# Loading the two rotary tables of a streaming encoder layer one sample sooner

## The chip, the cores and the metric

The kernel runs on one core of one Trainium2 chip. The metric is the time of one execution in device microseconds (us); lower is better. The engines are TensorE (PE in the rows, its weight loads PEld), VectorE (DVE), ScalarE (ACT), GpSimd (POOL) and SyncE (SP); SP and POOL do no arithmetic here, their instruction queues issue the transfers.

## The reference

One layer of a hybrid encoder is applied to a prompt of 512 frames and to 8 samples of 16 new frames each, with one set of weights. In order:

```python
x = x + 0.5 * swiglu(rms_norm(x, g1), w_in1, w_out1)
h = rms_norm(x, g_mix)
z = h @ w_in_mix            # rq rk rv rg | fq fk fv ff | two merge gates
q, k = rotary(rq, pos), rotary(rk, pos) * DK ** -0.5
o_ret = rms_norm(retention(q, k, rv, state)) * silu(rg)
o_fox = forgetting_attention(fq, fk, fv, log_sigmoid(ff), cache)
x = x + (g0 * (o_ret @ w_br_ret) + g1 * (o_fox @ w_br_fox)) @ w_out
x = x + 0.5 * swiglu(rms_norm(x, g2), w_in2, w_out2)
x = x + (p @ w_ple) * sigmoid(rms_norm(x, g_ple) @ w_ple_gate)
```

Each sample attends to 1024 cached frames of keys and values. The retention has 4 heads with keys of 128 and values of 256. `rotary` turns each pair of halves of a key or query by an angle that depends on its position:

```python
x1, x2 = xf[..., :half], xf[..., half:]
return concat([x1 * c - x2 * s, x1 * s + x2 * c])
```

## The kernel before

All 640 tokens (512 of the prompt, 128 of the samples) are kept with features on the 128 partitions and tokens along the free dimension. Weights arrive as raw f32 tiles (`raw`, 1 MB) and are split by `Parts.add` into a rounded part `wh` (ScalarE, line 282) and the rest `wl` (VectorE, line 283); three matmuls of 320 columns per weight block make up an f32 product (`mm`, line 205).

In the middle stage the input projection of the mixer is run as a list of units (`run_units`), and this work is the filler between the steps of the attention and of the retention: `fill(us)` lets the units go on for that much modelled matmul time. A unit of kind "s" (`MixSeven`) makes two blocks of 128 channels with seven products in three banks of PSUM, a, b and c (`pa`, `pg`, `pg`). Between its products, `after` combines the banks: after the third product VectorE subtracts a copy of bank a from bank b (line 819) and ScalarE copies bank b out (line 820), and only then may the fifth product write bank b again; VectorE subtracts that copy from bank c (line 824).

The main program around the change runs the eight samples one after the other (class `Sample`): their cached keys and values are loaded by `Sample.load` into tiles `kv` of 1 MB, of which there are four. The values of a sample are summed in `Sample.values`, one matmul group for each half of the cache (`pa<-kv,att`), scaled by VectorE at line 1335 and folded by a matmul (line 205, `pa<-sm,tmp`, copied out at line 1342). Behind the last sample come four heads of the retention (class `Retention`). `first_loads` and `loads` fetch a head's keys and queries from the scratch tensor `zdram` in DRAM, twice, once with the halves exchanged, six transfers for a head. They go into the `kv` tiles that the values of the seventh sample occupied, so they can't be issued before these are summed up. `rotate(0)` and `rotate(1)` then do the rotation for keys and queries with the two tables `tab`: two multiplications with the cosines and the sines (lines 1374 and 1375) and an addition (line 1376) each, on VectorE, over 640 columns.

The order in which instructions stand on each engine isn't the order of the program text. A scheduler sets it from its own model of how long things take; every engine then works off its row in order. Transfers issued by `load` go through the queue of SP, in that order too, and each of them also waits until the eighth one before it on that queue has landed. `load` itself is held back only by a scheduling hint: no sooner than `lead` of modelled matmul time before the place in the text.

The two tables are 128x640 in f32, 320 KB each, in `blk` tiles. Before the change they are loaded behind the last sample, after `until("rk")`, `fill(FILL_B)` and `pump(True)`.

Of the kernel before, what the change touches and what calls it, by code (L numbers as in the profile page):

```python
# [23 lines left out]
NB = 8  # L24
# [107 lines left out]
def kernel(  # L132
# [20 lines left out]
    def nm(base):  # L153
        uid[0] += 1
        return f"{base}_{uid[0]}"
# [3 lines left out]
    def blk(shape=(P, T), dt=F32, tag="blk"):  # L159
        n = 1  # L160
        for s in shape[1:]:
            n *= s
        assert n <= T
        return bp.tile(list(shape), dt, tag=tag, name=nm(tag), bufs=slots[tag])
# [16 lines left out]
    def tmp(shape=(P, H2), dt=F32):  # L181
        return bp.tile(list(shape), dt, tag="tmp", name=nm("tmp"), bufs=NTMP)
# [26 lines left out]
    def after(inst, name, why):  # L209
        tc.add_manual_dep(inst.ins, name, mybir.DependencyInfo(mybir.DependencyClass.NoSync, mybir.DependencyReason.SCHED_ONLY), reason=why)  # L210

    def load(out, in_, lead=LEAD):

        i = nc.sync.dma_start(out, in_)  # L214
        at = clock[0] - lead
        name = next((nm_ for c, nm_ in reversed(issued) if c <= at), None)
        if name is not None:
            after(i, name, "no tile taken too soon")
# [433 lines left out]
    with tc.manual_schedule(engines={mybir.EngineType.SP}):  # L652
        for q in range(KC // 2):
            cols = slice(q * 256, (q + 1) * 256)
            xi = big((P, TB, 256))
            n = P if q == 0 else 256
# [103 lines left out]
    def defer(us, thunk):  # L760
        uid[0] += 1
        heapq.heappush(deferred, (clock[0] + us, uid[0], thunk))

    def pump(everything=False):
        while deferred and (everything or deferred[0][0] <= clock[0]):
            heapq.heappop(deferred)[2]()
# [828 lines left out]
    def fill(us):  # L1595
        credit[0] += us
        while credit[0] > 0.0:
            at = clock[0]
            if next(feed, feed) is feed:
                clock[0] += credit[0]  # L1600
                credit[0] = 0.0
            credit[0] -= clock[0] - at
            pump()
# [24 lines left out]
    samples[0].load(samples[0].k, cache_k)  # L1628
    samples[0].load(samples[0].k, cache_k)
    fill(FILL_B)  # L1630
    for b in range(NB):
        defer(2.0, lambda: samples[b].loads(samples[b + 1] if b + 1 < NB else None))
        for n in range(8):
            samples[b].step(n)
            fill((FILL_S if b else FILL_S0) / 8)
    until("rk")
    fill(FILL_B)
    pump(True)
    tab = []
    for n in range(2):  # L1640
        r = blk()
        load(r, c_rope[n])
        tab.append(r)
    gqt, smt = tmp([P, RH, 2, 2 * L]), blk([P, RH, P])
    load(gqt, c_gq)
    load(smt, c_smask)
# [26 lines left out]
    for op in range(KC // 2):  # L1673
# [5 lines left out]
        for o in range(2):  # L1679
            n = 2 * op + o  # L1680
# [114 lines left out]
```

## Time and profile before

| | |
|---|---|
| median of 3 runs | 1624.56 us (1623.99 to 1625.74) |
| the profiled execution | 1622.67 us, its span 1620.9 us |
| TensorE busy | 1609.3 us, 99% of the span |
| VectorE / ScalarE busy | 1164.4 us (72%) / 731.5 us (45%) |
| mean granted clock of TensorE | 0.998 of full speed |

The profiled execution is 1.77 us longer than its span, which begins at its first instruction; it lies 1.9 us under the median of the runs. Since TensorE is busy nearly all the time, a change shows in the time where TensorE stands still, or where its clock is low, for longer or shorter than before. 0.2% of the time is 3.2 us.

### The profile page before, as it was taken

How to read it: one execution, taken by the hardware profiler on the slowest of the kernel's cores; microseconds unless marked ns; L12 is line 12 of the kernel's file. 1: busy time of each engine (PE TensorE's matmuls, PEld its weight loads, DVE VectorE, ACT ScalarE, POOL GpSimd, SP SyncE). 2: the span in 40 equal slices, each digit the busy share in tenths (PEclk: the TensorE clock that was granted, in tenths of full speed). 3: DMA queues.
4: the chain of work that ended last, by engine and by line, in shares of the span. 5: the costliest groups of instructions: out<-in, count | busy, mean ns of one | idle time of the engine just before them, and what ended most of it. 6: DMA issues, size and time to landing. Idle time of an engine off the chain costs nothing.

```text
span 1620.9 us, 30289 instructions
## 1 busy us (share of the span) xinstructions
PE 1609.3 (99%) x11979; PEld 1557.3 (96%) x11979; DVE 1164.4 (72%) x2472; ACT 731.5 (45%) x1536; POOL 94.5 (6%) x172
## 2 busy tenths in 40 slices
PE   9999999999999999999999999999999999999998
PEld 8999999999999888988889999999999999999998
DVE  6885786577777755777779886558884787578663
ACT  6552354244454444444434454435653355235432
POOL 0000000000011111000000010001000000000000
PEclk9999999999999999999999999999999999999999
DMA  7244233433542333577775676444234333433431
GB/s 249 78 131 139 96 93 131 145 101 94 178 130 97 111 115 133 209 281 269 279 259 179 202 260 247 151 135 155 79 101 164 100 91 124 144 111 90 172 123 46
DMA packets 205566, 242.88 MB, mean 150 GB/s; under 512 B 10176, under 2 KB 175984, under 8 KB 201328
## 3 DMA queue, kind: packets, MB, share of 16 engines
q1 hardware_dynamic: 193824, 200.07, 38.0%
q0 software_dynamic: 11392, 40.79, 6.3%
q8 instruction: 94, 1.54, 0.4%
q14 instruction: 48, 0.39, 0.1%
q10 hardware_dynamic: 208, 0.08, 0.0%
HBM read 194.89 MB, written 46.03 MB: 149 GB/s over the span
## 4 chain that ended last, share of the span: by engine, by line
PE 96%; DMA 2%; DVE 1%; ACT 1%; issue 0%; SPq 0%; DVEq 0%
PE pa L205 74%; PE pg L205 18%; PE pa L228 4%; DMA kv<-zdram 1%; DMA blk<-in_c_rope_dram 0%; DMA raw<-in_ffn_w_in_dram 0%; ACT tmp L533 0%; PE pg L228 0%; DVE wl L283 0%; ACT wh L282 0%; DMA kv<-in_x_prompt_dram 0%; SPq L214 0%; DVE kv L1487 0%; ACT blk L361 0%; DVE blk L1473 0%
## 5 line engine op out<-in xcount | busy, mean ns | idle before, releaser
L282 ACT CAST wh<-raw 128x512 fp32r<-128x512 f32 (+1 forms) x525 | 316.3, 613 | 506.7 <-PE pa L205 323.5
L205 PE MATMUL pa<-blk,wh 128*128 128x320 f32 x2344 | 511.1, 311 | 1.1 <-ACT wh L282 1.0
L283 DVE TENSOR_TENSOR wl<-raw,wh 128x512 fp32r<-128x512 f32 (+1 forms) x525 | 351.0, 678 | 107.0 <-ACT wh L282 103.6
L205 PEld LDWEIGHTS pa<-blk,wh 128*128 128x128 f32 x2344 | 388.2, 189 | 4.5 <-ACT wh L282 1.5
L205 PE MATMUL pa<-blk,wl 128*128 128x320 f32 x1172 | 344.4, 310 | 0.0
L205 PE MATMUL pa<-kv,wh 128*128 128x320 f32 x1344 | 251.5, 308 | 0.0
L205 PEld LDWEIGHTS pa<-blk,wl 128*128 128x128 f32 x1172 | 216.5, 189 | 0.5 <-DVE blk L830 0.4
L205 PEld LDWEIGHTS pa<-kv,wh 128*128 128x128 f32 x1344 | 210.6, 188 | 0.0
L205 PE MATMUL pg<-blk,wh 128*128 128x320 f32 x768 | 177.3, 316 | 0.2 <-DVE blk L830 0.2
L205 PE MATMUL pa<-blk,blk 128*128 128x320 f32 (+2 forms) x1064 | 168.3, 304 | 0.0
L205 PE MATMUL pa<-kv,wl 128*128 128x320 f32 x672 | 154.6, 308 | 0.0
L205 PEld LDWEIGHTS pa<-blk,blk 128*128 128x128 f32 (+1 forms) x1064 | 151.9, 183 | 0.1
L205 PE MATMUL pg<-wh,blk 128*128 128x256 f32 x768 | 147.6, 286 | 0.0
L205 PEld LDWEIGHTS pg<-blk,wh 128*128 128x128 f32 x768 | 128.2, 188 | 6.0 <-issue 2.4
L205 PEld LDWEIGHTS pg<-wh,blk 128*128 128x128 f32 x768 | 120.4, 188 | 5.1 <-issue 3.8
L205 PE MATMUL pg<-blk,wl 128*128 128x320 f32 x384 | 118.7, 309 | 0.0
L205 PEld LDWEIGHTS pa<-kv,wl 128*128 128x128 f32 x672 | 112.6, 188 | 0.0
L205 PE MATMUL pg<-wl,blk 128*128 128x256 f32 x384 | 108.7, 284 | 0.0
L283 DVE TENSOR_TENSOR blk<-raw,blk 128x512 fp32r<-128x512 f32 x82 | 56.3, 688 | 38.3 <-ACT blk L282 28.0
L205 PE MATMUL pa<-wh,blk 128*128 128x256 f32 (+1 forms) x432 | 82.4, 285 | 0.0
L282 ACT CAST blk<-raw 128x512 fp32r<-128x512 f32 x82 | 50.7, 621 | 62.5 <-DMA raw<-in_ffn_w_in_dram 48.8
L205 PEld LDWEIGHTS pg<-wl,blk 128*128 128x128 f32 x384 | 72.1, 188 | 1.9 <-issue 1.3
(287 smaller groups left out, 2205.1 us busy)
## 6 DMA issues: line engine op xcount, KB each, us to landing
raw<-in_ffn_w_in_dram SPq DMA_DIRECT2D x86, 512.0 KB, 4.8
raw<-in_w_in_mix_dram SPq DMA_DIRECT2D x25, 1024.0 KB, 5.8
raw<-in_ffn_w_out_dram SPq DMA_DIRECT2D x16, 1024.0 KB, 5.2
kv<-in_cache_fox_k_dram SPq DMA_DIRECT2D x16, 1024.0 KB, 7.1
kv<-in_cache_fox_v_dram SPq DMA_DIRECT2D x16, 1024.0 KB, 5.6
blk<-xd SPq DMA_DIRECT2D x48, 320.0 KB, 5.7
xd<-blk POOLq DMA_DIRECT2D x40, 320.0 KB, 2.8
zdram<-blk POOLq DMA_DIRECT2D x24, 320.0 KB, 3.4
```

The costliest lines, as they stand in the source:

```text
L205: i = nc.tensor.matmul(out, lhsT, rhs, start=start, stop=stop, **kw)
L228: tick(nc.tensor.transpose(out, in_, ident[: in_.shape[0], : in_.shape[0]]), 0.11)
L282: nc.scalar.copy(hi, src)
L283: nc.vector.tensor_tensor(lo, src, hi, op=ALU.subtract)
```

## The change

The two loads move from behind the samples to the start of the last turn of the loop over samples, ahead of that turn's `defer`:

```diff
     fill(FILL_B)
+    tab = []
     for b in range(NB):
+        if b == NB - 1:
+            for n in range(2):
+                r = blk()
+                load(r, c_rope[n])
+                tab.append(r)
         defer(2.0, lambda: samples[b].loads(samples[b + 1] if b + 1 < NB else None))
...
     until("rk")
     fill(FILL_B)
     pump(True)
-    tab = []
-    for n in range(2):
-        r = blk()
-        load(r, c_rope[n])
-        tab.append(r)
     gqt, smt = tmp([P, RH, 2, 2 * L]), blk([P, RH, P])
```

Nothing is added to the work or taken from it; the scheduler makes a new order from it on every engine from this place on.

The queue of SP around the first head's loads. Before, from the eighth sample's values on (`kv_10349` and `kv_10354` are the first head's keys and queries, `in_c_rope_dram` the tables):

```order
L214 DMA kv_9944<-in_cache_fox_v_dram 128x2048
L214 DMA kv_9946<-in_cache_fox_v_dram 128x2048
L214 DMA kv_10349<-zdram 128x640 x2
L214 DMA kv_10349<-zdram 64x640 x2
L214 DMA kv_10354<-zdram 64x640 x2
L214 DMA kv_10354<-vdram 128x1280
L265 DMA raw_10200<-in_w_in_mix_dram 128x8x256
L214 DMA att_10345<-in_c_rmask_dram 128x512
L214 DMA blk_10337<-in_c_rope_dram 128x640
L214 DMA blk_10339<-in_c_rope_dram 128x640
```

With the change, from the seventh sample's keys on, a little earlier in the same queue:

```order
L214 DMA kv_9394<-in_cache_fox_k_dram 128x2048
L214 DMA blk_9908<-in_c_rope_dram 128x640
L214 DMA kv_9655<-in_cache_fox_k_dram 128x2048
L214 DMA kv_9657<-in_cache_fox_v_dram 128x2048
L214 DMA kv_9659<-in_cache_fox_v_dram 128x2048
L214 DMA kv_9661<-in_cache_fox_k_dram 128x2048
L214 DMA blk_9910<-in_c_rope_dram 128x640
L265 DMA raw_9895<-in_w_in_mix_dram 128x8x256
L214 DMA kv_9948<-in_cache_fox_v_dram 128x2048
L214 DMA kv_9950<-in_cache_fox_v_dram 128x2048
L214 DMA kv_10349<-zdram 128x640 x2
```

The tables have moved from behind the first head's six loads to places in front of them, one of them by 13 rows; the six loads themselves keep their place behind the last sample's values.

VectorE, the first head's rotation (`wl_10369` belongs to the next raw tile, `wl_10257` to the one before it). Before:

```order
L424 TENSOR_TENSOR raw_9895<-raw_9895 128x4x128
L1374 TENSOR_TENSOR kv_10349<-kv_10349,blk_10337 128x640 x2
L1335 SCALAR_TENSOR_TENSOR tmp_10330<-pa_10293,ty_10188,sm 128x128
L1375 TENSOR_TENSOR kv_10349<-kv_10349,blk_10339 128x640
L1375 TENSOR_TENSOR kv_10354<-kv_10354,blk_10339 128x640
L283 TENSOR_TENSOR wl_10380<-raw_9895,wh_10379 128x512
L830 TENSOR_TENSOR blk_10280<-pg_10206,blk_10280 128x320
L283 TENSOR_TENSOR wl_10412<-raw_9895,wh_10411 128x512
L1376 TENSOR_TENSOR kv_10349<-kv_10349 128x640
L1376 TENSOR_TENSOR kv_10349<-kv_10349,kv_10354 128x640
```

With the change, where `wl_10261`, `wl_10369` and line 819 are what `wl_10257`, `wl_10369` and line 819 were before:

```order
L1374 TENSOR_TENSOR kv_10349<-kv_10349,blk_9908 128x640
L1307 TENSOR_REDUCE ty_10192<-ty_9913 128x1
L1374 TENSOR_TENSOR kv_10349<-kv_10349,blk_9908 128x640
L1308 RECIPROCAL ty_10192<-ty_10192 128x1
L283 TENSOR_TENSOR wl_10261<-raw_9556,wh_10260 128x512
L1375 TENSOR_TENSOR kv_10349<-kv_10349,blk_9910 128x640
L1342 COPY tmp_10225<-pa_10223 128x64
L1375 TENSOR_TENSOR kv_10354<-kv_10354,blk_9910 128x640
L1376 TENSOR_TENSOR kv_10349<-kv_10349 128x640
L1376 TENSOR_TENSOR kv_10349<-kv_10349,kv_10354 128x640
L283 TENSOR_TENSOR wl_10369<-raw_9895,wh_10368 128x512
L819 TENSOR_TENSOR pg_10210<-pg_10210,tmp_10245 128x320
```

The six instructions of the rotation stood behind `wl_10369`, line 819 and seven more; now they stand ahead of all of these, the first of them right behind the `MEMSET` of line 1298.

TensorE, the values of the last sample (`pa_10293` before, `pa_10297` now) and the fifth product of the unit into bank b (`pg_10206`, `pg_10210`). Before:

```order
L205 MATMUL pa_10293<-kv_9944,att_10253 32x128 x16
L205 MATMUL pa_10293<-kv_9946,att_10272 32x128 x16
L205 MATMUL pa_10293<-blk_5123,tmp_10291 32x128 x4
L205 MATMUL pg_10206<-blk_5242,wh_10224 128x320
L205 MATMUL pg_10206<-blk_5243,wh_10224 128x320
```

With the change:

```order
L205 MATMUL pa_10297<-kv_9948,att_10257 32x128 x16
L205 MATMUL pg_10210<-blk_5242,wh_10228 128x320
L205 MATMUL pg_10210<-blk_5243,wh_10228 128x320
L205 MATMUL pg_10210<-blk_5242,wl_10229 128x320
L205 MATMUL pg_10210<-blk_5513,wh_10228 128x320
L205 MATMUL pa_10297<-kv_9950,att_10276 32x128 x16
L205 MATMUL pa_10297<-blk_5123,tmp_10295 32x128 x4
```

Four matmuls of the fifth product now stand between the two halves of the values.

## Rows read from the trace of the kernel before

**Rows 1.** The page: span, and busy time of each engine.

```profile
span 1620.9 us, 30289 instructions
...
PE 1609.3 (99%) x11979; PEld 1557.3 (96%) x11979; DVE 1164.4 (72%) x2472; ACT 731.5 (45%) x1536; POOL 94.5 (6%) x172
```

**Rows 2.** Waits, TensorE, whole span: us in total, times, longest.

```profile
PE pa L205 <- DVE tmp L1335: 2.6, 1, 2.6
```

**Rows 3.** Stretches of 5 us: busy time (x instructions), PEclk, DMA share, GB/s.

```profile
825.00:830.00 5.00, 4.16 (x44) 3.70 (x32) 0.97 (x3) 1.86 (x3) 0.00 (x0) 1.00 1.05 389
830.00:835.00 5.00, 3.25 (x13) 3.25 (x14) 5.00 (x9) 0.00 (x0) 0.00 (x0) 0.69 1.07 383
```

**Rows 4.** Timeline, TensorE, 818 to 845: start, us, instruction [idle before <-releaser].

```profile
823.30 1.96 PE L205 MATMUL pa<-kv,att 128*32 128x128 f32 x64
...
831.75 0.57 PE L205 MATMUL pa<-sm,tmp 128*128 128x64 f32 x2 [2.59 <-DVE tmp L1335]
832.09 0.88 PE L205 MATMUL pa<-blk,wh 128*128 128x320 f32 x2
...
835.39 0.46 PE L205 MATMUL pg<-blk,wh 128*128 128x320 f32 x2
```

**Rows 5.** Timeline, VectorE, around the first head's rotation.

```profile
825.19 0.69 DVE L424 TENSOR_TENSOR raw<-raw 128x512 f32<-128x512 f32 x1
829.88 1.56 DVE L1374 TENSOR_TENSOR kv<-kv,blk 128x640 f32<-128x640 f32 x2 [4.00 <-DMA blk<-in_c_rope_dram]
831.36 0.34 DVE L1335 SCALAR_TENSOR_TENSOR tmp<-pa,ty,sm 128x128 f32<-128x128 f32 x1
```

**Rows 6.** The chain of waits, 795 to 860: start, us, what.

```profile
813.95 6.03 DMA kv<-zdram
...
822.05 7.81 DMA blk<-in_c_rope_dram
...
835.55 1.76 PE pg L205 x12
```

**Rows 7.** Timeline, queue of SP, 690 to 860.

```profile
776.55 5.36 SPq L214 DMA_DIRECT2D kv<-in_cache_fox_k_dram  x2
...
792.51 0.33 SPq L214 DMA_DIRECT2D kv<-in_cache_fox_k_dram  x1
...
813.95 4.23 SPq L214 DMA_DIRECT2D kv<-zdram  x6
...
824.54 0.48 SPq L214 DMA_DIRECT2D kv<-in_state_ret_dram  x1
825.84 4.53 SPq L214 DMA_DIRECT2D kv<-zdram  x4
```

**Rows 8.** DMA issues at 814.9 and 816.6 (size, us to landing); zdram's transfers, 800 to 880.

```profile
kv<-zdram SPq DMA_DIRECT2D x1, 160.0 KB, 6.9
kv<-zdram SPq DMA_DIRECT2D x1, 160.0 KB, 7.4
DMA to landing us min/median/max: 2.4/6.1/10.3
```

**Rows 9.** Timeline, VectorE, 811 to 837.

```profile
815.37 0.17 DVE L1298 MEMSET tmp<- 128x128 f32 x1
...
817.50 0.69 DVE L283 TENSOR_TENSOR wl<-raw,wh 128x512 fp32r<-128x512 f32 x1 [0.93 <-ACT wh L282]
818.57 0.23 DVE L1342 COPY tmp<-pa 128x64 f32<-128x64 f32 x1 [0.37 <-PE pa L205]
820.87 0.69 DVE L283 TENSOR_TENSOR wl<-raw,wh 128x512 fp32r<-128x512 f32 x1 [2.08 <-ACT wh L282]
821.48 0.49 DVE L819 TENSOR_TENSOR pg<-pg,tmp 128x320 f32<-128x320 f32 x1
...
834.69 0.81 DVE L1376 TENSOR_TENSOR kv<-kv 128x640 f32<-128x640 f32 x1
```

**Rows 10.** Timeline, ScalarE, 811 to 837.

```profile
822.37 0.45 ACT L820 COPY tmp<-pg 128x320 f32<-128x320 f32 x1
```

## The prediction

> **What bounds the kernel now.** I read the busy times of the page first: TensorE works for 1609.3 of the 1620.9 us [rows 1], so only what it loses can be won. Then its waits: nearly all that it loses once the program runs is one wait of 2.6 us, for VectorE's line 1335 [rows 2]. Then the windows, to see its stage: between 825 and 835 TensorE is idle for 0.84 and 1.75 us, and in the second stretch its mean granted clock is 0.69 [rows 3], so besides standing still it runs for a while at the lower of its two levels, 1.2 instead of 2.4 GHz. The timeline of TensorE gives both losses. It stands for 2.59 us until 831.75. The twelve matmuls of 320 columns from 832.09 to 835.39 then take 3.30 us [rows 4], while twelve such matmuls right behind them take 1.76 [rows 6], so the low clock costs 1.54 more. Together the place costs **4.13 us**, 0.25% of the time.
>
> The timeline of VectorE tells why: it has nothing from the end of line 424 (825.19 + 0.69 = 825.88) to 829.88, and the releaser is the landing of a table [rows 5]. Line 1335, which TensorE wants, stands behind the first two multiplications and has to wait too. The chain agrees: the load of the table, issued at 822.05, lands 7.81 us later, and the piece ahead of it is the load of the first head's keys from `zdram`, issued at 813.95 and landing 6.03 us later, at 819.98 [rows 6]. This second number decides the forecast: 819.98 is the earliest time at which the rotation could start with the tables already there.
>
> **The change part by part.** *The tables' loads.* With the change the first goes behind the load issued at 776.55 and the second behind the one at 792.51 [rows 7]. The buffers that they take are free by then: the matmul that last reads the second one's stands right ahead of its place in TensorE's order, and SP waits there for TensorE anyway. So the tables land well before 815, and the wait of 4.00 us for them is gone. Two issues fewer stand behind the six loads of the head, two more ahead of them; the six still wait for the values of the seventh sample, and I leave them where they are, from 813.95 to 818.18 [rows 7]. Up to 815.37 I cost everything at nothing: all the loads that the tables are put ahead of wait for TensorE or VectorE at their own places.
>
> *The rotation's new place.* What the diff doesn't show is VectorE's order. The six instructions now stand right behind the `MEMSET` of 815.37 [rows 9], ahead of the weight part of 817.50, that of 820.87 and line 819 of 821.48. VectorE works in order, so at 815.54 it stops for the first head's keys, which land at 819.98. That is a wait of 4.44 us, in place of the 4.00 removed, and now everything up to line 819 is queued behind it.
>
> *When line 819 is done.* Durations from start to start: a multiplication 0.74 (two in 831.36 - 829.88 [rows 5]), an addition the same (it shows 0.81 by itself [rows 9]), a weight part 0.61 (821.48 - 820.87 [rows 9]), each of the three small ones 0.2 (0.23 shown [rows 9]). The landings of loads two to six are bounded: the second by the issue at 822.05 and the sixth by the one at 824.54, since each issue of this queue waits until the eighth one before it has landed [rows 6, 7]; the third and the fifth are shown, 814.9 + 6.9 = 821.8 and 816.5 + 7.4 = 823.9 [rows 8].
> - Latest: first multiplication 819.98 to 820.7; second, with load two at 822.05, to 822.8; small one and weight part to 823.6; third to 824.35; small one; fourth, with load six at 824.54, to 825.3; two additions to 826.8; weight part to 827.4; line 819 (0.49 [rows 9]) to 827.9.
> - Earliest: load two at once, so the second ends at 821.65, the third at 823.2; the fourth has to wait for load five and ends at 824.65; additions to 826.1, weight part to 826.75, line 819 to 827.25.
>
> Then ScalarE copies bank b (line 820, 0.45 [rows 10]): **827.7 to 828.35**. I take 828.2, near the late end, because load five at 823.9 is close to the bound of load six, and every hand-over between engines adds a little.
>
> *What TensorE does meanwhile.* Its cover is what it has ahead of the fifth product. It begins the values of the eighth sample at 823.30, 1.96 us for both halves [rows 4]; with the change the fifth product stands between the halves, so it stops after the first, at 824.28. Nothing it needs before then comes from behind the rotation: line 1335 of the seventh sample stands ahead of it, and so do the weight parts of the products until there. So it stands from 824.28 to 828.2, **3.9 us** (3.4 to 4.1 by the two ends).
>
> *The clock.* An idle time of 2.59 us sent it to its lower level [rows 3, 4], so one of 3.9 should too; I charge the same 1.54. Bounds: 0, if it happens not to fall, and 2.3, if the low stretch grows with the idle time (1.54 x 3.9 / 2.59).
>
> *Behind it.* The old wait goes: line 1335 has no table in front of it any more, and VectorE reaches it some 4 us after line 819, at about 832, when TensorE still has eight matmuls of the fifth and twelve of the seventh product ahead. The next raw tile is issued by SP only after the weight part of 817.50, so that and what follows in the queue goes out some 5 us later; none of it is wanted before 840, except the second head's keys (second rival).
>
> *Sum.* Removed 2.59 + 1.54 = 4.13; added 3.9 + 1.54 = 5.44; net **+1.3 us**. Ends: 3.4 idle with no low clock gives -0.7, 4.1 idle with 2.4 of low clock +2.4. Against the profiled execution this is 1622.67 + 1.3 = 1624.0. That execution lies 1.9 under the median of the runs, so for the median I forecast 1624.56 + 1.3 = **1625.9 us**, with an own range of 1623.0 to 1627.8 (the ends, and the 0.9 by which the runs stray). A difference of less than 0.2%, 3.2 us, counts as no change.
>
> **The rivals.** *One: the wait vanishes, as one would hope.* If the six loads landed quickly, the rotation would be over before TensorE runs out. The shortest transfer of this tensor here landed after 2.4 us [rows 8]. The keys would then be there at 816.35 and the sixth load by 817.2 + 2.4 = 819.6; fourth multiplication, additions, weight part, line 819 and line 820 would end at 819.6 + 0.74 + 1.48 + 0.61 + 0.49 + 0.45 = 823.4, before 824.28. TensorE would not stand at all: 1624.56 - 4.13 = **1620.4**, faster by 0.25%. Against it: 6.03, 6.9 and 7.4 us are shown for these very loads [rows 6, 8], and they keep their place behind the same traffic. The Trainium skill, page "DMA: Bandwidth & Descriptors", section "Anatomy of one DMA", fits a transfer's time as 2.0 us and its bytes by 436 GB/s (a fit for the other way of making descriptors), which by my estimate is 2.75 us for 320 KB. By that rule this rival would be the forecast; the trace doesn't agree, with 6.03 us for the first of them.
>
> *Two: a second wait makes it slower.* The second head's keys go into the tile that the second half of the last values frees. Before, they were issued at 825.84 [rows 7]; now those values end only after 828.2 + 1.1 (four matmuls at the slow rate of 3.30 / 12) + 0.98, so the issue moves to about 830.4. The multiplication that wants them now stands singly ahead of the raw sum of line 434 and a weight part, and VectorE comes to it at about 836 (fifteen instructions, 7.6 us, behind line 819, a little for TensorE's products). Landing 10.3 us after issue, the longest shown [rows 8], means 840.7; then come two multiplications by this table, the raw sum, a weight part, one multiplication by the other table and line 836, some 3.9 us, to 844.6. TensorE gets to the product that waits for line 836 at about 843.0 (72 matmuls at 1.76 / 12, some 2.5 for values and transposes, 1.54 for the clock, from 828.2). That is 1.6 us more idle and, if the clock falls again, 1.54 more: 1624.56 + 1.3 + 3.1 = **1629.0**. It decides from a landing of 8.7 us on. For it: the second head's loads take that long before the change. Against it: the tables no longer share the queue with them, and the other late loads have had a start.
>
> *Three: it comes to nothing*, 1624.6: the old wait and the new one are equal within a few tenths, because the first half of the values or the landings stray by one. Nothing speaks against that but the sum's 1.3.
>
> **How the numbers follow.** The forecast has 0.65, the first rival 0.14, the second 0.13, the third 0.08. Faster by over 0.2% is the first rival: 0.14. Slower by over 0.2% is most of the second and the top of the forecast's range: 0.14. The rest, 0.72, is no change. The range reaches from 1622.0, below the forecast's own end, to 1629.0 so as to hold the second rival, and leaves out the first.
>
> **What would show it.** In the profile of the changed kernel: no wait for the tables anywhere; VectorE's longest idle time of this stage before its first line 1374, ended by `kv<-zdram` at about 820 and not later than 821; TensorE idle once for 3 to 4 us up to about 828, put down to ScalarE's line 820 or VectorE's line 819; its clock low in 830 to 835 again; line 1335 no releaser of TensorE any more. I am wrong if TensorE has no wait over 1 us between 815 and 845 (first rival), if it has a second one near 843 (second), or if the keys land before 818.

## The result, and the profile after

| | before | changed |
|---|---|---|
| median of 22 runs each | 1623.30 us | 1626.12 us |
| lowest and highest | 1620.60 to 1625.74 | 1623.27 to 1631.01 |
| ratio, 95% interval | | 1.0018 (1.0011 to 1.0024) |

The changed kernel is 0.18% slower, inside the 0.2% that the prediction called no change. Later runs of the same kernel gave 1.0022 (1.0013 to 1.0031) and 1.0024 (1.0014 to 1.0034). Two of the eleven executions of one later kernel, held_sooner, took 3188 us at full clock where its other nine took 1621.5 to 1623.9, and its ratio below is that of the nine. The forecast of 1625.9 us is met within 0.3 us, in part by luck: it was 1.3 us on a base of 1624.56, the median of three runs, while the median of 22 is 1623.30, and against that the change costs 2.8 us (1.8 to 3.9 by the interval). The reasons given for it don't hold: what follows shows that the place which was to get worse got better, and that the time went 100 to 160 us further on.

The page of the changed kernel; this execution took 1623.27 us, the shortest of the 22:

```profile
span 1621.5 us, 30281 instructions
...
PE 1609.2 (99%) x11979; PEld 1554.9 (96%) x11979; DVE 1163.8 (72%) x2472; ACT 730.4 (45%) x1536; POOL 94.5 (6%) x172
```

The waits of TensorE in it, whole span (us in total, times, longest), the two that answer to [rows 2]:

```profile
PE pg L205 <- ACT tmp L820: 2.0, 2, 1.1
PE pa L205 <- DMA kv<-in_state_ret_dram: 1.3, 1, 1.3
```

The wait for line 1335 is gone. In its place stand two for line 820 and one for a load that the prediction never speaks of. The stretch that answers to the second of [rows 3] (busy us of PE, PEld, DVE, ACT and POOL, each with its instructions, PEclk, DMA share, GB/s):

```profile
830.00:835.00 5.00, 5.00 (x36) 5.00 (x36) 3.41 (x8) 2.05 (x4) 1.29 (x2) 1.00 1.03 330
```

TensorE works all through this stretch at 2.4 GHz, where its mean clock was 0.69 of full speed before. VectorE and TensorE at the place (start, us, instruction, idle time before and its releaser):

```profile
815.70 0.17 DVE L1298 MEMSET tmp<- 128x128 f32 x1
817.86 0.82 DVE L1374 TENSOR_TENSOR kv<-kv,blk 128x640 f32<-128x640 f32 x1 [1.99 <-issue]
...
823.49 0.82 DVE L1376 TENSOR_TENSOR kv<-kv,kv 128x640 f32<-128x640 f32 x1
824.23 0.69 DVE L283 TENSOR_TENSOR wl<-raw,wh 128x512 fp32r<-128x512 f32 x1
824.83 0.49 DVE L819 TENSOR_TENSOR pg<-pg,tmp 128x320 f32<-128x320 f32 x1
```

```profile
823.63 1.08 PE L205 MATMUL pa<-kv,att 128*32 128x128 f32 x32
825.83 0.55 PE L205 MATMUL pg<-blk,wh 128*128 128x320 f32 x2 [1.12 <-ACT tmp L820]
...
931.44 0.57 PE L205 MATMUL pg<-blk,wh 128*128 128x320 f32 x2 [0.90 <-ACT tmp L820]
...
977.63 0.59 PE L205 MATMUL pa<-kv,tmp 128*32 128x256 f32 x2 [1.30 <-DMA kv<-in_state_ret_dram]
```

VectorE does stop behind the `MEMSET` for the first head's keys, and TensorE does stop between the halves of the last values, but for 1.12 us and not 3.9. The first keys' load, issued at 814.28, lands at 817.8 instead of 820, and the later loads of the head are sooner too. The first load's size and time to landing, then two pieces of the chain of waits between 815 and 827:

```profile
kv<-zdram SPq DMA_DIRECT2D x1, 320.0 KB, 3.5
```

```profile
817.61 4.25 DMA kv<-zdram
...
822.01 0.83 DVE kv L1375
```

The load that the chain to line 820 hangs on is the head's sixth, issued at 817.61 and landing at 821.86; the fourth multiplication waits for it. The prediction had it land by 824.54. The rows of TensorE at 931.44 and 977.63 are new. At 977.63 TensorE waits for the state of the last head, 1 MB from `in_state_ret_dram`, which feeds that head's eight small products with the samples' states (`values_s`).

To see what the whole stage takes, two marks serve that every kernel here has: the start of the last sample's values and the first product of the next stage with `ones`. From one to the other (busy us of PE behind the length of the stretch), before and changed:

```profile
823.30:1132.26 308.96, 305.79 (x2149) 291.36 (x2149) 235.82 (x483) 139.28 (x279) 29.81 (x53) 0.99 0.57 196
```

```profile
823.63:1133.20 309.57, 305.58 (x2149) 289.49 (x2149) 234.79 (x482) 139.65 (x281) 29.80 (x53) 1.00 0.56 192
```

TensorE does the same 2149 instructions in both. Before, it is idle for 308.96 - 305.79 = 3.17 us, 2.59 of them at the place of [rows 4], and 1.54 of the busy time is the low clock there. Now it is idle for 3.99 us, 1.12 at the place and 2.87 behind it. So the place gained 2.59 + 1.54 - 1.12 = 3.01 us; the waits behind it rose by 2.87 - 0.58 = 2.29, and the same work kept TensorE busy for 305.58 - (305.79 - 1.54) = 1.33 us longer. The sum is +0.61, which is 309.57 - 308.96. Waits and busy time behind the place stand against the gain there.

### The profile page after: what moved, and what is told of

Same layout as the page of the kernel before. It is cut to its first block, busy times and chain, and to the rows that moved or that the text cites. A ratio compares the mean times of both kernels' runs of the same rounds, so it can differ in the third digit from the quotient of the medians.

```text
span 1621.5 us, 30281 instructions
## 1 busy us (share of the span) xinstructions
PE 1609.2 (99%) x11979; PEld 1554.9 (96%) x11979; DVE 1163.8 (72%) x2472; ACT 730.4 (45%) x1536; POOL 94.5 (6%) x172
## 3 DMA queue, kind: packets, MB, share of 16 engines
q8 instruction: 94, 1.54, 0.4%
## 4 chain that ended last, share of the span: by engine, by line
PE 93%; DMA 3%; DVE 2%; ACT 1%; SPq 1%; issue 0%; DVEq 0%; ACTq 0%
PE pa L205 72%; PE pg L205 17%; PE pa L228 4%; DMA kv<-in_state_ret_dram 1%; DMA kv<-zdram 1%; DVE wl L283 1%; DMA raw<-in_w_br_fox_dram 0%; DMA raw<-in_ffn_w_in_dram 0%; PE pg L228 0%; SPq L650 0%; ACT wh L282 0%; DMA kv<-in_x_prompt_dram 0%; DVE kv L1376 0%; SPq L660 0%; DVE kv L1487 0%
```

## The experiments

Two theories were set against each other. **A, the place:** the loss is TensorE's wait for line 820 behind the rotation, as predicted, and this one execution shows little of it. **B, the tail:** the place has improved, and the loss is behind it, where the scheduler's order is another one for 190 us more. By the two traces, TensorE's row of the changed kernel first differs from that of before behind the first half of the last values, at 824.2 us, and is the same again only from 1018 us on. Up to there, 214 matmuls of 320 columns stand behind the first product with the last head's states in the kernel before, 226 in the changed one.

All ratios are against runs of the kernel before on the same chip. The times in the column on the tail are those of the run itself.

| run | rotation | tail | ratio | 95% interval |
|---|---|---|---|---|
| again, other_tail (the changed kernel) | ahead of line 819 | changed | 1.0022, 1.0024 | 1.0013 to 1.0034 |
| two_sooner | ahead of line 819 | a third | 1.0008 | 1.0000 to 1.0017 |
| tail_held | ahead of line 819 | changed, states late | 1.0014 | 1.0006 to 1.0023 |
| late_states | ahead of line 819 | a fourth | 0.9982 | 0.9974 to 0.9991 |
| cos_early | half of it | before's from 931 us | 0.9991 | 0.9983 to 1.0000 |
| held | where it was | before's from 860 us | 0.9981 | 0.9972 to 0.9989 |
| held_sooner | a row earlier | a fifth | 0.9996 | 0.9986 to 1.0005 |
| held_tail_of_change | where it was | changed from 865 us | 1.0033 | 1.0020 to 1.0045 |
| held_late_states | where it was | a sixth | 1.0001 | 0.9992 to 1.0010 |
| held_tables_late | behind line 1335 | changed from 911 us | 1.0016 | 1.0008 to 1.0025 |

**again.** The changed kernel as it is.

> The changed kernel once more, for a second profile. Theory A (the place): what the change costs is TensorE's wait for line 820 behind the rotation; the profile at hand shows only 1.12 us of it because the first keys landed early there. Then a second profile has 2 to 4 us at that place, more where the keys land later, and the time is again 2 to 4 us over the kernel before. Theory B (the tail): the place costs 1 us in nearly every execution, and the loss is made up of the waits near 930 and 977 that the new order brings further on; then the second profile has 1 us for line 820 near 825 and 1 to 3 us for the load of the last head's state near 977.

This execution took 1626.36 us, next to the median of 1626.38. TensorE:

```profile
826.41 0.57 PE L205 MATMUL pg<-blk,wh 128*128 128x320 f32 x2 [1.84 <-ACT tmp L820]
...
978.60 0.66 PE L205 MATMUL pa<-kv,tmp 128*32 128x256 f32 x2 [1.50 <-DMA kv<-in_state_ret_dram]
979.18 0.90 PE L205 MATMUL pg<-blk,wh 128*128 128x320 f32 x2
...
982.49 0.59 PE L205 MATMUL pa<-kv,att 128*128 128x256 f32 x2
```

and between the marks and in the stretch behind the state's load:

```profile
823.49:1135.69 312.20, 307.14 (x2149) 290.89 (x2149) 235.51 (x483) 139.68 (x281) 29.78 (x53) 0.99 0.56 191
...
980.00:985.00 5.00, 5.00 (x27) 4.90 (x26) 2.68 (x5) 4.02 (x10) 0.54 (x1) 0.76 0.20 77
```

The place costs 1.84 us, at full clock. Behind 978.60 the clock is down: the twelve matmuls from 979.18 to 982.49 take 3.31 us where twelve take 1.76 [rows 6], so 1.55 more. Against before: the place -2.59 - 1.54 + 1.84 = -2.29; waits behind it 3.22 - 0.58 = +2.64; the low clock +1.55; busy without either low clock 305.59 - 304.25 = +1.34. The sum is +3.24, and 312.20 - 308.96 is 3.24. B holds; A's "2 to 4 us at that place" fails narrowly, and the time is over before's in spite of it.

**held.** The tables as early as in the change; a scheduling hint, which moves nothing but the scheduler's choice, keeps the rotation back:

```diff
-            nc.vector.tensor_tensor(r, r, tab[0], op=ALU.mult)
...
+            at = clock[0] - 6.0
+            behind = next((nm_ for c, nm_ in reversed(issued) if c <= at), None)
+            for i in (
+                nc.vector.tensor_tensor(r, r, tab[0], op=ALU.mult),
+                nc.vector.tensor_tensor(w, w, tab[1], op=ALU.mult),
+                nc.vector.tensor_tensor(r, r, w, op=ALU.add),
+            ):
+                if self.hd == 0:
+                    after(i, behind, "no sooner than the products around it")
```

> Tables as early as in the change, but the first head's rotation is kept by a scheduling hint where it stood before, behind line 424; TensorE's order of the last head's state products is that of the kernel before. Both theories: no wait for the tables, none for the keys, no wait of TensorE over 0.5 us between 815 and 845, its clock full there; 3.5 to 4.5 us under the kernel before, a ratio of 0.9972 to 0.9978. If it is not faster by at least 2 us, the place is not worth what the profile of before puts on it.

0.9981, 3.4 us by the medians (1620.00 to 1623.37): a little under the 3.5 expected (0.9978, which lies inside the interval). It is the fastest version here, level with late_states below. VectorE (the lines of the rotation are three higher, 1377 to 1379), TensorE's stretch that was at 0.69 before, and the time between the marks:

```profile
824.77 0.69 DVE L424 TENSOR_TENSOR raw<-raw 128x512 f32<-128x512 f32 x1
825.38 0.82 DVE L1377 TENSOR_TENSOR kv<-kv,blk 128x640 f32<-128x640 f32 x1
```

```profile
830.00:835.00 5.00, 5.00 (x36) 5.00 (x36) 3.56 (x8) 0.95 (x2) 1.29 (x2) 1.00 0.96 319
...
822.88:1128.61 305.73, 305.09 (x2149) 290.36 (x2149) 235.51 (x483) 138.63 (x279) 29.79 (x53) 1.00 0.57 195
```

Where [rows 5] have 4.00 us of waiting ahead of the rotation, none is left, and TensorE idles for 0.64 us in all. Idle time and low clock are 3.17 + 1.54 - 0.64 = 4.07 us less than before, nearly the 4.13 that the profile of before put on the place; TensorE is busy for 0.84 us longer, so that 3.23 us are left. The early tables pay if they don't carry the rotation with them. TensorE's row is that of before again from 860 us on.

**held_tail_of_change.** held, with the hint's reference also given to the first head's steps 2 to 8 (2 us back), which makes the later order that of the change:

```diff
+        if gate[0] is not None:
+            after(inst, gate[0], "no sooner than the products around it")
...
+            if hd == 0 and 2 <= at <= 8:
+                gate[0] = next((nm_ for c, nm_ in reversed(issued) if c <= clock[0] - 2.0), None)
             step()
+            gate[0] = None
```

> The first place of held (rotation behind line 424, TensorE's row as there up to row 5292) with the tail of the changed kernel: from row 5405 on, to the end, TensorE's row is the changed kernel's word for word. Theory B: nothing lost near 825, but the tail's waits are back (1 us near 930, 1.3 to 1.5 us for the last head's state near 977) with its longer busy time: 3 to 5 us over held, 1.0000 to 1.0012 of the kernel before. Theory A: as held, 0.9981.

1.0033, more than B expected. The rows (line 822 is line 820, 826 is 824 here), the stretch behind the state's load and the marks:

```profile
837.37 0.74 PE L230 MATMUL pa<-sm,kv 128*128 128x128 f32 x5 [1.58 <-DVE kv L1381]
...
846.13 0.56 PE L207 MATMUL pg<-blk,wh 128*128 128x320 f32 x2 [2.41 <-DVE pg L826]
...
933.87 0.57 PE L207 MATMUL pg<-blk,wh 128*128 128x320 f32 x2 [0.88 <-ACT tmp L822]
...
980.42 0.59 PE L207 MATMUL pa<-kv,tmp 128*32 128x256 f32 x2 [1.67 <-DMA kv<-in_state_ret_dram]
```

```profile
980.00:985.00 5.00, 4.58 (x19) 3.93 (x19) 2.05 (x4) 3.95 (x9) 0.00 (x0) 0.69 0.63 230
...
822.69:1137.58 314.89, 306.86 (x2149) 290.55 (x2149) 236.27 (x483) 138.71 (x279) 29.80 (x53) 0.99 0.55 190
```

Two things are in it. From 900 on the waits are those of the changed kernel, row for row (0.88 at 934 for 0.90, 1.67 for the state for 1.30 to 1.50, and the low clock behind it as in again). But the seam between the two orders, up to 846.13, brought some 4 us of waits (4.65, of which held has 0.45) that the changed kernel doesn't have.

The tail can still be priced by itself. Counted from the first mark, the first 755 matmuls are the same set in each of these kernels, by names and shapes, so from the 756th, near 930 us, to the second mark each has the same 1393 matmuls left (the rows count two or three more, which reach over the ends). The stretch between these two in the kernel before, in held, in the changed kernel and in this one:

```profile
931.26:1132.26 201.00, 201.00 (x1395) 194.25 (x1394) 140.66 (x281) 95.75 (x187) 20.77 (x38) 1.00 0.55 191
```

```profile
927.61:1128.61 201.00, 201.00 (x1395) 194.23 (x1394) 140.59 (x281) 95.53 (x187) 20.75 (x38) 1.00 0.55 191
```

```profile
928.54:1133.20 204.66, 202.46 (x1396) 194.77 (x1395) 142.00 (x283) 96.20 (x187) 21.56 (x40) 1.00 0.54 188
```

```profile
930.97:1137.58 206.61, 204.06 (x1396) 195.94 (x1395) 142.04 (x283) 96.18 (x187) 21.55 (x40) 0.99 0.54 187
```

With the order of before it takes 201.0 to 201.5 us in four executions (also before_again and cos_early), with that of the change 204.6 to 206.6 in five (also again, other_tail and held_tables_late), whatever happened at the place. Up to its start the changed kernel is ahead of the one before, by 3.05 us in the first execution, 2.27 in again and 0.69 in other_tail; behind it, it loses 3.66, 5.51 and 3.79. That is theory B.

**late_states.** The change with the same hint on the first head's steps, the rotation left ahead of line 819. A first try, **other_tail** (steps 2 to 4, 8 us back), was to do this:

> The changed kernel with TensorE's row as in it up to 101 matmul rows behind the first place (row 5306), so with the rotation ahead of line 819; a hint on the first head's transposes and scores alone makes the scheduler's order from there on another one, in which the last head's eight products with its states stand together, with 48 matmuls of 320 columns behind the first of them as in the kernel before. Theory B (what the change loses, it loses behind the first place): 1 to 3 us for line 820 near 825, no wait for the last head's state, so 1 to 3 us under the kernel before, 0.9982 to 0.9994, if the new order has no other waits of its own. Theory A (it is lost at the first place): 1.0015 to 1.0025, as the changed kernel.

Its hint changed no row on any engine: it is the changed kernel a third time, 1.0024, with the same three waits, two of them shown here, and one of 1.04 us at 883.65 (line 822 is line 820):

```profile
825.95 0.57 PE L207 MATMUL pg<-blk,wh 128*128 128x320 f32 x2 [1.73 <-ACT tmp L822]
...
979.63 0.59 PE L207 MATMUL pa<-kv,tmp 128*32 128x256 f32 x2 [1.43 <-DMA kv<-in_state_ret_dram]
```

Then with steps 2 to 8, 2 us back:

> What the run before this one (other_tail) was meant to be; its hint had changed no engine's row, so it was the changed kernel a third time. Here the hint does move them: TensorE's row is that of the changed kernel up to row 5306, some 80 matmul rows behind the first place, and from there on another, in which the last head's eight products with its states stand together with 48 matmuls of 320 columns behind the first of them, as in the kernel before. Theory B: 1 to 3 us for line 820 near 825, no wait for the last head's state, so 1 to 3 us under the kernel before, 0.9982 to 0.9994, if the new order has no other waits of its own; each that it has is to be added. Theory A: 1.0015 to 1.0025, as the changed kernel.

0.9982 with the rotation where the change puts it. TensorE in its profiled execution (1623.24 us, the longest of the 12, against a median of 1621.06):

```profile
826.55 0.56 PE L207 MATMUL pg<-blk,wh 128*128 128x320 f32 x2 [2.35 <-ACT tmp L822]
...
846.77 0.90 PE L207 MATMUL pg<-blk,wh 128*128 128x320 f32 x2 [2.27 <-DVE pg L826]
```

```profile
823.12:1132.26 309.14, 302.07 (x2150) 289.73 (x2150) 235.50 (x484) 139.91 (x281) 30.23 (x54) 0.99 0.57 193
```

TensorE waits for line 820 longer than in the changed kernel, 2.35 us, and the kernel is still 0.18% faster than before: A falls. It isn't the clean case that B hoped for, since this tail has a wait of its own at 846.77, with the low clock behind it, and TensorE is busy for 302.07 us, 3.5 less than in the change, for the same work.

**tail_held.** The change, with the last head's eight products alone kept back by a hint:

```diff
-                    mm(po[pr * 32:(pr + 1) * 32, :DV], self.qg[:, pr, j, :], self.st[:, 2 * pr + j, :], False, j == 1, skip_group_check=True)
+            behind = next((nm_ for c, nm_ in reversed(issued) if c <= clock[0] - 2.0), None)
...
+                    i = mm(po[pr * 32:(pr + 1) * 32, :DV], self.qg[:, pr, j, :], self.st[:, 2 * pr + j, :], False, j == 1, skip_group_check=True)
+                    if self.hd == RH - 1:
+                        after(i, behind, "the state lands late")
```

> The changed kernel, its first place as it is (rotation ahead of line 819); only the last head's eight products with its sample states are kept back in TensorE's order by a hint, so that 48 matmuls of 320 columns stand behind the first of them, about as in the kernel before. Theory B (the tail costs): no wait for the state's load, 1 to 2 us for line 820 near 825, 1 us near 930: 2 to 4 us under the changed kernel, so 0.9985 to 1.0003 of the kernel before. Theory A (the place costs): as the changed kernel, 1.0018 to 1.0022.

1.0014: by the ratio a miss of both, and no clear gain, since its interval and those of the change overlap. TensorE in its profiled execution (1623.09 us, the shortest of the 12):

```profile
825.39 0.56 PE L205 MATMUL pg<-blk,wh 128*128 128x320 f32 x2 [1.04 <-ACT tmp L820]
...
980.28 0.56 PE L205 MATMUL pg<-blk,wh 128*128 128x320 f32 x2 [0.95 <-DVE blk L1553]
```

The wait for the state is gone, and 0.95 us for line 1553 (1550 without the edit) stands in its place. One wait of the tail isn't the tail.

**two_sooner.** `if b == NB - 2` instead of `NB - 1`.

> The tables loaded one turn sooner still (at the seventh sample). The rotation stands as in the changed kernel, one row later; the last head's state products come some 2 us later in TensorE's order than there. Theory A: as the changed kernel, 2 to 4 us over the kernel before (1.0018), with the wait for line 820 near 825. Theory B: the tail's wait is smaller or gone, so 0 to 1 us from the kernel before (1.0000).

1.0008, between the two. VectorE and TensorE, with the next stretch:

```profile
819.64 0.82 DVE L1374 TENSOR_TENSOR kv<-kv,blk 128x640 f32<-128x640 f32 x1 [2.96 <-DMA kv<-zdram]
```

```profile
827.51 0.57 PE L205 MATMUL pg<-blk,wh 128*128 128x320 f32 x2 [2.96 <-ACT tmp L820]
```

```profile
830.00:835.00 5.00, 5.00 (x37) 5.00 (x36) 4.37 (x10) 2.14 (x4) 0.53 (x1) 1.00 1.04 343
```

Here the first keys landed late, at 819.6, nearly as predicted for the change, and TensorE stood for 2.96 us; the clock stayed full all the same.

**cos_early.** Only `c_rope[0]` moved up.

> Only the cosine table is loaded early, the sine table as late as before; the order of the last head's state products is that of the kernel before. The two multiplications by the cosines move ahead of line 819, those by the sines stay ahead of line 1335 and wait for their table. Both theories: VectorE waits 3 to 4 us for the sine table, TensorE 2 to 3 us for line 1335 as before; little at line 820. Theory B: 0.9990 to 1.0008 of the kernel before. Theory A, by which the keys in front of line 819 are what costs: another 1 to 2 us at line 820, 1.0005 to 1.0020.

0.9991, at the low end of B. The half of the rotation that has its table moves, the other half waits as before:

```profile
830.84 1.56 DVE L1375 TENSOR_TENSOR kv<-kv,blk 128x640 f32<-128x640 f32 x2 [4.68 <-DMA blk<-in_c_rope_dram]
```

```profile
832.71 0.43 PE L205 MATMUL pa<-sm,tmp 128*128 128x64 f32 x2 [3.28 <-DVE tmp L1335]
```

TensorE loses more at the place than in any other kernel, and the kernel isn't slower than before: the place alone doesn't set the time.

**held_tables_late.** The kernel before with the hint of held (2 us back), so that the rotation comes behind line 1335.

> The kernel before, tables as late as ever, only the first head's rotation kept back by the hint until behind line 1335; TensorE's order of the last head's state products comes out as that of the changed kernel. Theory A: the wait of 4 us goes though no table lands sooner, and nothing else costs much: 3.5 to 4.5 us under the kernel before (0.9975). Theory B: the same gain, less the 2.4 us that the tail costs in the profile of the changed kernel: 1 to 2 us under (0.9990), with a wait of 1 to 3 us for the last head's state near 975.

1.0016, missed by both. The table is still waited for, but by nobody else:

```profile
829.39 0.83 DVE L1377 TENSOR_TENSOR kv<-kv,blk 128x640 f32<-128x640 f32 x1 [0.92 <-DMA blk<-in_c_rope_dram]
...
836.02 0.83 DVE L1377 TENSOR_TENSOR kv<-kv,blk 128x640 f32<-128x640 f32 x1 [1.68 <-DMA kv<-zdram]
...
837.37 0.48 DVE L836 TENSOR_TENSOR blk<-pg,blk 128x320 f32<-128x320 f32 x1
```

```profile
837.91 0.56 PE L205 MATMUL pg<-blk,wh 128*128 128x320 f32 x2 [1.59 <-DVE blk L836]
...
979.86 0.59 PE L205 MATMUL pa<-kv,tmp 128*32 128x256 f32 x2 [1.68 <-DMA kv<-in_state_ret_dram]
```

Ordering alone removes the wait of 2.59 us. But line 836, which TensorE waits for, stands behind a multiplication for the second head, and VectorE waits 1.68 us for that head's keys; and the kernel comes with the tail of the change.

**held_sooner** has `clock[0] - 5.0` for `6.0`; **held_late_states** is held with step hints from 4 us back.

> As held, but the hint lets the rotation start 1 us sooner: the first place is as free as there (rotation behind line 423), but the scheduler's order from there on is another, and the last head's first state product has 84 matmuls of 320 columns behind it instead of 60. Theory B: nothing lost near 825, but 1.5 to 3 us for the state's load near 975 and some more for smaller waits ahead of it: 2 to 4 us over held, 0.9995 to 1.0010 of the kernel before. Theory A: as held, 0.9981.

> The first place of held with a third order behind it: the last head's eight state products together and late, and the small state products of all heads in 10 groups on TensorE instead of 16 (late_states has 10 too, and there TensorE was busy 302.1 us between the last values and the next stage, against 304.3 in the kernel before without its low clock, 305.1 in held). Theory B: no wait near 825, busy time 2 to 3 us under held, other waits 0 to 3 us: 4 to 7 us under the kernel before, 0.9957 to 0.9976. Theory A: as held, 0.9981.

0.9996 and 1.0001. held_sooner is as B said, though not by the waits that B named: it has no wait for the state, 1.30 us idle in all, and TensorE is busy for 308.22 us, the longest here. held_late_states is a miss of 4 us or more: it is less busy as expected (303.15), but has waits of its own, the longest of them

```profile
919.58 1.18 PE L230 MATMUL pa<-sm,att 128*128 128x128 f32 x4 [2.62 <-DVE att L1455]
```

and a low clock behind it.

**before_again.** The kernel before, unchanged.

> The kernel before for a second profile: whether the 6.03 us of the first keys' load and the low clock behind the 2.59 us of idle time are there in each execution. If the 6.03 us are the rule of this order, the keys land at 819.5 to 820.5 again; if they are one draw of a range, at 817 to 820. VectorE waits 3.5 to 4.5 us for the first table either way.

The wait and the low clock (0.76 in the stretch from 830) are there again; the keys are not late. They land at 813.80 + 3.87 = 817.67, and VectorE stands for 4.13 us ahead of its first multiplication, until 829.87 (the profile puts the end of this wait down to the load of a mask, not to the table). TensorE, the stretch, and the first two loads of the head (size, us to landing):

```profile
831.75 0.43 PE L205 MATMUL pa<-sm,tmp 128*128 128x64 f32 x2 [2.73 <-DVE tmp L1335]
```

```profile
830.00:835.00 5.00, 3.25 (x15) 3.25 (x16) 5.00 (x9) 0.16 (x1) 0.00 (x0) 0.76 1.05 363
```

```profile
kv<-zdram SPq DMA_DIRECT2D x2, 320.0 KB, 3.9
```

The 6.03 us of [rows 6] were one draw of a range.

## Why the prediction came out right for the wrong reason

**The tables.** Right: they land before 815, nothing waits for them, and line 1335 releases no stalled TensorE any more.

**VectorE at 815.5.** Right in kind and wrong in size. The prediction has "at 815.54 it stops for the first head's keys, which land at 819.98. That is a wait of 4.44 us"; it stopped at 815.87 for 1.99 us. The step that failed is the price of the head's loads, taken from one profile: 6.03 us for the first, and bounds from the same rows for the others. In the fourteen profiles there are now, the first of the head's two loads of 320 KB whose landing is shown takes 3.4 to 6.0 us, in six of them 3.9 or less: 3.5 in the changed kernel, 3.9 in before_again, 3.6 in held_tables_late, 5.5 in two_sooner, whether the tables are early or late. The row I used was the longest of all. The first rival's 2.4 us, by the shortest transfer of the tensor, was too short. The Trainium skill, "DMA: Bandwidth & Descriptors", section "Anatomy of one DMA", gives 2.75 us by the estimate in the prediction; no profile comes down to it, though ten of the fourteen lie nearer to it than to 6.03. Nor is 819.98 the number that "decides the forecast": line 819 hangs on the sixth load, which landed at 821.86 in the changed kernel and at 822.10 in again, for 823.9 to 824.54 in the prediction.

**Line 819 and line 820.** Predicted to end at 827.25 to 827.9 and at 828.2; line 819 starts at 824.83, and TensorE goes on at 825.83. The stop itself was read rightly from the order: predicted from 824.28, it came at 825.83 - 1.12 = 824.71, at exactly that matmul. So "3.9 us (3.4 to 4.1 by the two ends)" was 1.12, 1.84 and 1.73 in three executions of the changed kernel, all outside the bounds.

**The clock.** "An idle time of 2.59 us sent it to its lower level [rows 3, 4], so one of 3.9 should too": behind the wait for line 820 near 825 it fell in none of six profiles, not even behind 2.96 us (two_sooner). Behind the wait for line 1335 it fell each time.

**The sum at the place.** Predicted +1.3 us; measured -3.01 (first execution) and -2.29 (again). Of the first rival's -4.13 the place gave more than half.

**What lies behind.** This is the term that the sum puts at nothing: +3.6 us in the first execution, +5.5 in again (waits 2.64, low clock 1.55, busy time 1.34) and in other_tail, where the clock stayed full (waits 3.68, busy time 1.84). The prediction's part "Behind it" follows the new order to 840 and the second rival to 844.6. The order differs up to 1018 us, and the prediction looks at rows only around the place. Two errors of opposite sign, 3.6 us too dear at the place and 5.5 us missing behind it, came out 2 us apart, less than the 0.2% that I had called no change. That, and the base of 1624.56, is luck.

**The rivals.** The first is what held makes of the change. The second named a wait near 843 for line 836, behind the second head's keys. In the changed kernel VectorE does wait for these keys (1.59 us until 834.82), but TensorE doesn't wait for line 836; in held_tables_late it does (1.59 us at 837.91). The third's 0 was the sum's size, by accident.

What stays open: why the scheduler's later choices differ so far from one rotation moved, and how much of the 5.5 us each of the tail's three parts would give back alone. tail_held shows that undoing one wait brings the next.

## What to carry to other kernels

Where a scheduler writes the order, an edit that frees one resource early changes the model's clock and with it every later choice: compare each engine's row until it is the same again, not only around the edit, and give what lies between a term or a wider range. If moved work pays by itself, pin what it would drag along to its old place (held: 0.9981, with 0.9972 to 0.9989, where the change alone is 1.0018). And a transfer's duration read once in a profile is one draw: look at its likes, and at a second execution, before a wait is worked out to a tenth. To price a tail by itself, find a point up to which two kernels have done the same set of products, and compare the times from there.

## What the hardware showed that I had not expected

- The idle time alone doesn't say whether TensorE's clock falls. Behind line 1335, 2.59, 2.73 and 3.28 us of idle time were each followed by the low level (1.2 GHz); behind line 820, 2.96 and 2.35 us were not. For the same wait for the last head's state it fell behind 1.50 us (again) and 1.67 (held_tail_of_change), and not behind 1.30 (the changed kernel), 1.43 (other_tail) and 1.68 (held_tables_late). Line 824 (826 in these two) went both ways near 846: the clock fell behind 2.27 us (late_states) and not behind 2.41 (held_tail_of_change). What tells these cases apart isn't in the views.
- The same matmuls between the marks kept TensorE busy for 302.07 to 308.22 us, by their order. In the rows of TensorE the products with `pa<-kv,tmp`, nearly all of them the small ones of the four heads' states, stand in 16 groups in the kernel before and in held (304.25 without the low clock, and 305.09 us), in 18 in held_sooner (308.22), in 10 in late_states and held_late_states (302.07 and 303.15, low clock included). That would fit a price for each change between them and the large products, but no run isolates it, and it isn't what the change lost: the changed kernel has 15 groups and is busy for 305.58 us.
- The last head's state, 1 MB, lands 14.6 to 18.3 us after its issue near 962 in the thirteen profiles that show it, the second head's state, as large and issued near 866, after 5.0 to 5.5: between 960 and 980 the DMA engines move some 400 GB/s without a break, while from 865 to 870 of the kernel before, where the earlier one was issued, they moved 38. That fits a wait behind other transfers; no run isolates it. TensorE asks for the last state's product at 976.3 in the changed kernel, for 980.6 before, and it lands at 977.5: the product can only wait.
